# A hybrid encoder trunk: a head's eight groups of half-width products in one visit, and side work between the two products of a pair

## The chip, the cores and the metric

The kernel runs on one core of one Trainium2 chip. The metric is the device time of the whole program in microseconds (us), the median of several runs. The engines are named as the profile names them: PE (matrix products; PEld is its weight load), DVE (vector), ACT (scalar), POOL (general purpose), and SP, which issues most of the DMAs.

## The reference

The reference is a two-layer encoder trunk on 256 tokens of width 2048. Layer 0 mixes tokens with a bidirectional mLSTM, layer 1 with a bidirectional gated linear recurrence (HGRN2); each mixer is followed by a gated MLP of width 5504 with a convolution of width 3. The change touches the second mixer, whose core is this:

```python
def _hgrn_chunk(s_st, xs):
    q, k, lf, v = xs
    b = jnp.cumsum(lf, axis=2)
    rel = jnp.where(lower[:, :, None], b[:, :, :, None, :] - b[:, :, None, :, :], -jnp.inf)
    attn = jnp.einsum('bhtsk,bhsk->bhts', jnp.exp(rel) * q[:, :, :, None, :], k)
    o = jnp.einsum('bhts,bhsv->bhtv', attn, v) + jnp.einsum('bhtk,bhkv->bhtv', q * jnp.exp(b), s_st)
...
def hgrn_mixer(hn, w_in, lb, head_g, w_out):
    p = hn @ w_in
    q, i, g, f_f, f_b = jnp.split(p, [B_F, B_F + B_V, B_F + 2 * B_V, 2 * B_F + 2 * B_V], axis=-1)
    log_f = jnp.logaddexp(log_lb, log_1mlb + jax.nn.log_sigmoid(f))
    k = (1.0 - lb) * jax.nn.sigmoid(-f)
...
    y = hgrn_direction(q, k_f, lf_f, v) + fl(hgrn_direction(fl(q), fl(k_b), fl(lf_b), fl(v)))
    y = head_rmsnorm(y, head_g, B_HEADS) * jax.nn.silu(g)
    return y @ w_out
```

It has 16 heads of width 128. In words: a token's output is a sum over all earlier tokens (and, in the other direction, all later ones) of q times k times the product of the gates between the two tokens, times v.

## The kernel before

**The stream.** `stream` (line 151) runs through a list of chunks of weights. For each piece of 1024 columns `split_weights` has a DMA bring the float32 weights (`raw`), ACT round them to a high part `wh` (line 146) and DVE subtract to get the low part `wl` (line 147). Four buffers hold each part, and three pieces are prepared ahead. A chunk of kind "fm" has two output tiles f = 0, 1 and a contraction index k from 0 to 15 (or 21, 20); for each k and f there is a **pair** of products: `wh` against 512 columns (activations' high and low part, line 197) and `wl` against 256 columns (line 198). A chunk of kind "tm" has three products of 512 columns for each half of the tokens (lines 187 to 189). After each k the stream calls `side.tick`, with 0.65 units in "fm" and 1.3 in "tm".

**The side jobs.** `Side` (line 82) holds Python generators. A tick adds to a clock; a generator whose due time has come is run to its next `yield`, which names the units to the next step (2.4 for most heads of the second mixer, 1.9 for the last two and where nothing is named). The instructions that it issues thereby stand in program order at that tick. The framework that builds the program then lays out each engine's order by program order and by when its own model of times has the operands ready; an instruction whose operands are late moves behind others. Once built, each engine's order is fixed. A **visit** is a run of side products on PE between two products of the stream.

**A head of the second mixer.** `head` (line 596) waits until the head before it has set `done`, then goes through seven levels h = 1, 2, ..., 64. At each level DVE copies ("gathers") the blocks of k and q that matter there into two tiles `km` and `qm` of 256 columns (line 608), multiplies k and q by gates (lines 629, 630), and POOL multiplies neighbouring gates (line 635). Each level's tiles give one **group** of four half-width products (64 columns of weights, 64 columns streamed, line 616), and plain float32 takes two passes for each. An eighth group comes from `ks` and `q` (line 641). The groups fill quarters of a PSUM tile `pd`; with seven levels and one for `ks`, the eight groups take two tiles. Before the change they come in two visits: after level 4 (`li == 2`) the groups of levels 1, 2, 4 and of `ks`, whose results ACT copies (line 642) and DVE merges by mask (line 644) into `AD`; and after the last level the groups of levels 8 to 64, merged by line 650 and copied into `AT` (lines 654, 655), directly followed by two full-width products `pd<-QK` (lines 657, 658), copied by line 659. One step later AT meets V in eight products `py` (line 670). `done` is set in the second visit.

**Around it.** For every four heads there are three "fm" chunks, a "tm" chunk (V), three "fm" chunks and a "tm" chunk (the output gate). `finish` (line 677) scales four heads' outputs, transposes each on PE (`pz`, line 691) and writes them to `yb0` to `yb15`, in the buffers `yt0` to `yt15`, which the output projection reads. PSUM has four tiles for the stream and four (`aux`) for the side work. `km` and `qm` have five buffers each (`MIX`).

Of the kernel before, what the change touches and what calls it, by code (L numbers as in the profile page):

```python
# [8 lines left out]
F32 = mybir.dt.float32  # L9
# [6 lines left out]
P = 128  # L16
T = 256
D = 2048
KT = D // P
# [25 lines left out]
MIX = 5  # L45
FIRST = (0, 1, 2, 4, 7, 10, 13, 16)

HALF = 64
LEVELS = (1, 2, 4, 8, 16, 32, HALF)
# [4 lines left out]
def trunk_kernel(ctx, tc, xT, pp_d, cst_d, w_first, w_aq, w_ak, w_av, w_ao, w_aout,  # L54
                 w_bq, w_bv, w_bg, w_bout, w_up, w_down, out, mscr, stop=9):
    nc = tc.nc
    act, dve, pool, pe = nc.scalar, nc.vector, nc.gpsimd, nc.tensor

    keep = ctx.enter_context(tc.tile_pool(name="keep", bufs=1))
# [18 lines left out]
    def aux(name):  # L78
        return psa.tile([P, 512], F32, tag="aux", name=name)
# [30 lines left out]
    side = Side()  # L110
# [40 lines left out]
    def stream(chunks):  # L151
        pieces = split_weights(chunks)
        ready = []

        def fetch():
            p = next(pieces, None)
            if p is not None:
                ready.append(p)

        for _ in range(LOOK):  # L160
            fetch()
        for ch in chunks:
            if ch.before:
                ch.before()
            ps = [psm.tile([P, 512], F32, tag="mm", name="mm") for _ in range(3 if ch.kind == "first" else 2)]
            k = 0
            while k < ch.nk:
                fetch()
                wh, wl, n = ready.pop(0)
                if ch.last:  # L170
                    for f in range(2):
                        for kk in range(n):
                            x, c = ch.x(k + kk), kk * 256 + f * P
                            terms = ((wh, 0), (wl, 0), (wh, T))
                            for i, (w, o) in enumerate(terms):
                                pe.matmul(ps[f][:, 0:T], w[:, c:c + P], x[:, o:o + T], start=(k + kk == 0 and i == 0),  # L176
                                          stop=(k + kk == ch.nk - 1 and i == 2))
                    k += n
                    continue
                for kk in range(n):  # L180
                    x = ch.x(k)
                    st, sp = k == 0, k == ch.nk - 1
                    if ch.kind != "fm":
                        c = slice(kk * 512, (kk + 1) * 512)
                        for t in range(2):
                            xh, xl = x[:, t * P:(t + 1) * P], x[:, T + t * P:T + (t + 1) * P]
                            pe.matmul(ps[t], xh, wh[:, c], start=st, stop=False)  # L187
                            pe.matmul(ps[t], xh, wl[:, c], start=False, stop=False)  # L188
                            pe.matmul(ps[t], xl, wh[:, c], start=False, stop=sp)  # L189
                        if ch.kind == "first":  # L190
                            pe.matmul(ps[2], wh[:, 512:512 + P], x, start=st, stop=False)
                            pe.matmul(ps[2][:, 0:T], wl[:, 512:512 + P], x[:, 0:T], start=False, stop=sp)
                        side.tick(1.3)
                    else:
                        for f in range(len(ps)):
                            c = kk * ch.width + f * P
                            pe.matmul(ps[f], wh[:, c:c + P], x, start=st, stop=False)  # L197
                            pe.matmul(ps[f][:, 0:T], wl[:, c:c + P], x[:, 0:T], start=False, stop=sp)  # L198
                        side.tick(0.325 * len(ps))
                    k += 1  # L200
            ch.done(ps)

# [16 lines left out]
    def late(dst, src):  # L219
        tc.keep_in_program_order(nc.sync.dma_start(dst, src))  # L220
# [315 lines left out]
    def hgrn(norm, nxt):  # L536
        YT = [None] * KT
        stack = ExitStack()
        box = {}

        def begin():
            mp = box["mp"] = stack.enter_context(tc.tile_pool(name="hg", bufs=1))
            late(cst[:, C_LV:], cst_d[:, C_LV:])
            lb = box["lb"] = mp.tile([P, KT], F32, name="lb")
            oml = box["oml"] = mp.tile([P, KT], F32, name="oml")
            t0 = mp.tile([P, 2, KT], F32, name="t0")
            t1 = mp.tile([P, KT], F32, name="t1")
            raw = pp[:, OFF["lb"]:OFF["lb"] + 2 * KT].rearrange("p (a b) -> p a b", a=2)
            dve.tensor_tensor(t1, raw[:, 0], raw[:, 1], ALU.max)
            for i in range(2):  # L550
                dve.tensor_tensor(t0[:, i], raw[:, i], t1, ALU.subtract)
            act.activation(t0, t0, AF.Exp)
            dve.tensor_tensor(t1, t0[:, 0], t0[:, 1], ALU.add)
            dve.reciprocal(t1, t1)
            for i in range(2):
                dve.tensor_tensor(t0[:, i], t0[:, i], t1, ALU.mult)
            dve.tensor_tensor(lb, t0[:, 0], t0[:, 1], ALU.add)
            dve.tensor_tensor(lb, lb, t0[:, 0], ALU.subtract)
            dve.tensor_scalar(oml, lb, -1.0, 1.0, ALU.mult, ALU.add)

        def blocks(z, h, a, b):
            v = z[:, 0:2 * (T + h)].rearrange("k (p x) -> k p x", p=2)[:, :, a:b]
            return v.rearrange("k p (m j) -> k m p j", j=2 * h)[:, :, :, 0:h]

        def gview(g, n, start, h):
            v = g[:, start:start + 2 * (n - 1)].rearrange("k (p x) -> k p x", p=2)[:, :, 0::2]
            return v.rearrange("k p m -> k m p").unsqueeze(3).broadcast_to([P, n // 2, 2, h])
# [28 lines left out]
        def head(hd):  # L596
            mp = box["mp"]
            st = heads[hd]
            while hd and "done" not in heads[hd - 1]:
                yield 0.3  # L600
            QZ, KZ = st["QK"][:, 0:640], st["QK"][:, 512:1152]
            q, ks, G = st["q"], st["ks"], st["G"]
            AT = mp.tile([P, 4, P], F32, tag="AT", bufs=2, name="AT")
            AD = mp.tile([P, 2, HALF], F32, tag="AD", bufs=2, name="AD")

            def gather(z, h, tag):
                m = mp.tile([P, T], F32, tag=tag, bufs=MIX, name=tag)
                dve.tensor_copy(m.rearrange("k (m p j) -> k m p j", p=2, j=h), blocks(z, h, 0, T))
                return m

            def product(pd, k, q, flip=0):

                for b in range(4):
                    o, c = b % 2 * HALF, b // 2 * HALF
                    e = b ^ flip
                    pe.matmul(pd[o:o + HALF, c:c + HALF], k[:, b * HALF:(b + 1) * HALF], q[:, e * HALF:(e + 1) * HALF],  # L616
                              start=True, stop=True)

            def both(ps):
                return ps.rearrange("p (a b) -> p a b", a=2)  # L620

            step = SPREAD if hd < BH - 2 else STEP
            mask = [cst[:, C_LV + i * HALF:C_LV + (i + 1) * HALF].bitcast(I32).unsqueeze(1).broadcast_to([P, 2, HALF])
                    for i in range(6)]
            ms, n = [(gather(KZ, 1, "km"), gather(QZ, 1, "qm"))], T
            yield step
            for li, h in enumerate(LEVELS):
                qa, ka = blocks(QZ, h, 0, T), blocks(KZ, h, 0, T)
                dve.tensor_tensor(ka, ka, gview(G, n, 1, h), ALU.mult)  # L629
                dve.tensor_tensor(qa, qa, gview(G, n, n + 1, h), ALU.mult)  # L630
                if h < HALF:
                    ms.append((gather(KZ, 2 * h, "km"), gather(QZ, 2 * h, "qm")))
                    n //= 2
                    G2 = mp.tile([P, 3 * n], F32, tag=f"G{h}", bufs=2, name="G2")
                    pool.tensor_tensor(G2, G[:, 0:6 * n:2], G[:, 1:6 * n:2], ALU.mult)
                    G = G2
                if li == 2:
                    pd = aux("pd")
                    for i in (2, 1, 0):
                        product(pd[:, (i + 1) * P:(i + 2) * P], *ms[i])  # L640
                    product(pd[:, 0:P], ks, q)
                    act.copy(AD, both(pd[:, 0:P]))
                    for i in range(3):
                        dve.copy_predicated(AD, mask[i], both(pd[:, (i + 1) * P:(i + 2) * P]))
                yield step
            pd = aux("pd")
            for i in (6, 5, 4, 3):
                product(pd[:, (i - 3) * P:(i - 2) * P], *ms[i], i == 6)
            for i in (3, 4, 5):
                dve.copy_predicated(AD, mask[i], both(pd[:, (i - 3) * P:(i - 2) * P]))  # L650
            src = both(pd[:, 3 * P:4 * P])
            st["done"] = True
            for o in (0, HALF):
                act.copy(AT[o:o + HALF, 0::3, HALF - o:P - o], src[o:o + HALF])
                act.copy(AT[o:o + HALF, 0::3, o:o + HALF], AD[o:o + HALF])
            pd = aux("pd")
# [6 lines left out]
            V, j = st["qd"]["V"], hd % 4  # L663
# [229 lines left out]
```

## Time and profile before

| what | number |
|---|---|
| median of 3 runs | 2452.22 us (2452.00 to 2452.59) |
| the profiled execution's own time | 2451.01 us |
| its span, first to last instruction | 2449.2 us |
| granted PE clock, mean | 0.998 |
| second mixer with its projection, by the windows view | 1150 to 1664 us |
| in that stretch: PE, DVE, ACT, POOL busy | 512.8, 438.1, 263.2, 129.2 us of 514 |
| half-width products (line 616), records | 896 + 128 |

The table's stretch of 514 us is the only part of the program in which the heads of the second mixer run. A PE record begins when PE starts on a matmul and ends when its last result is out; records overlap, so the distance from one start to the next is what a matmul takes of PE's time, not the record's length. The timeline merges equal neighbours into one line: the first column is the start of the first, the second the time to the end of the last, and the count stands behind x.

### The profile page before, as it was taken

The page shows a single profiled execution, that of the slowest core. Times are in us where ns is not written, and L with a number is a line of the kernel's source. Part 1 is how long each engine was busy: PE and PEld are TensorE (multiplying, and loading weights), DVE is VectorE, ACT ScalarE, POOL GpSimd, SP SyncE. Part 2 cuts the span into 40 slices and gives each one's busy share as a digit, 9 for nine tenths or more (in the row PEclk, how much of TensorE's full clock was granted, in tenths as well). Part 3 has the DMA queues.
Part 4 walks back from the last instruction along what each step waited for, and adds up shares of the span by engine and source line. Part 5 has one row for each costly group of instructions (what it writes and reads, how often), then busy time and mean ns, then how long its engine had stood idle before and what let it go on. Part 6 is the DMA issues. An engine that isn't in the chain of part 4 may idle for free.

```text
span 2449.2 us, 36986 instructions
## 1 busy us (share of the span) xinstructions
PE 2432.1 (99%) x14462; PEld 2108.3 (86%) x14462; DVE 1759.7 (72%) x2943; ACT 1221.2 (50%) x1890; POOL 267.4 (11%) x325
## 2 busy tenths in 40 slices
PE   9999999999999999999999999999999999999998
PEld 7888888888888888888888888888888888888887
DVE  7766577777656777668888888888777755677754
ACT  6655455444444444445455555545544444444443
POOL 0100032000000000122222222224000000000022
PEclk9999999999999999999999999999999999999999
DMA  7654555555556555555544445445555555555553
GB/s 261 189 179 160 184 187 184 191 191 191 179 189 202 189 189 189 181 183 191 172 160 168 162 165 172 160 156 201 186 191 191 186 189 194 189 189 189 185 190 125
DMA packets 65920, 448.88 MB, mean 183 GB/s; under 512 B 7616, under 2 KB 8256, under 8 KB 15568
## 3 DMA queue, kind: packets, MB, share of 16 engines
q1 hardware_dynamic: 63936, 443.03, 54.2%
q0 software_dynamic: 800, 2.16, 0.6%
q8 instruction: 113, 1.85, 0.3%
q10 hardware_dynamic: 1008, 1.32, 0.2%
q14 instruction: 63, 0.52, 0.1%
HBM read 444.32 MB, written 2.16 MB: 182 GB/s over the span
## 4 chain that ended last, share of the span: by engine, by line
PE 98%; DVE 1%; ACT 0%; issue 0%; DMA 0%; SPq 0%; POOL 0%; DVEq 0%; POOLq 0%
PE mm L197 53%; PE mm L198 26%; PE mm L187 5%; PE mm L189 5%; PE mm L188 5%; PE pd L616 1%; PE pn L440 1%; PE mm L176 1%; PE py L670 1%; DVE wl L147 0%; PE S L426 0%; PE pd L657 0%; DMA raw<-in_w_first 0%; DVE QK L629 0%; PE pz L691 0%
## 5 line engine op out<-in xcount | busy, mean ns | idle before, releaser
L147 DVE TENSOR_TENSOR wl<-raw,wh 128x1024 fp32r<-128x1024 f32 (+1 forms) x864 | 1047.5, 1214 | 546.4 <-ACT wh L146 533.5
L197 PE MATMUL mm<-xt,wh 128*128 128x512 f32 x3776 | 1319.5, 395 | 0.0
L146 ACT CAST wh<-raw 128x1024 fp32r<-128x1024 f32 (+1 forms) x864 | 884.1, 1025 | 833.2 <-PE mm L197 481.5
L198 PE MATMUL mm<-xt,wl 128*128 128x256 f32 x3776 | 1049.9, 278 | 0.0
L197 PEld LDWEIGHTS mm<-xt,wh 128*128 128x128 f32 x3776 | 708.3, 188 | 164.3
L198 PEld LDWEIGHTS mm<-xt,wl 128*128 128x128 f32 x3776 | 710.1, 188 | 0.8
L197 PE MATMUL mm<-g,wh 128*128 128x512 f32 x1334 | 462.6, 394 | 0.0
L198 PE MATMUL mm<-g,wl 128*128 128x256 f32 x1334 | 369.5, 277 | 0.0
L197 PEld LDWEIGHTS mm<-g,wh 128*128 128x128 f32 x1334 | 250.1, 188 | 58.0
L198 PEld LDWEIGHTS mm<-g,wl 128*128 128x128 f32 x1334 | 250.5, 188 | 0.0
L187 PE MATMUL mm<-wh,xt 128*128 128x512 f32 x512 | 201.9, 398 | 3.1 <-ACT xt L204 2.5
L188 PE MATMUL mm<-wl,xt 128*128 128x512 f32 x512 | 201.5, 394 | 0.4 <-DVE wl L147 0.4
L189 PE MATMUL mm<-wh,xt 128*128 128x512 f32 x512 | 200.6, 393 | 0.0
L209 ACT COPY b<-mm 128x256 f32<-128x256 f32 x237 | 87.6, 370 | 172.2 <-PE mm L198 172.2
L243 POOL TENSOR_TENSOR acc<-hx 128x256 f32<-128x256 f32 x4 | 4.8, 1203 | 1238.3 <-DVE hx L312 1238.3
L187 PEld LDWEIGHTS mm<-wh,xt 128*128 128x128 f32 x512 | 95.7, 188 | 23.3 <-ACT xt L204 2.7
L189 PEld LDWEIGHTS mm<-wh,xt 128*128 128x128 f32 x512 | 96.5, 188 | 19.9
L188 PEld LDWEIGHTS mm<-wl,xt 128*128 128x128 f32 x512 | 96.5, 188 | 19.4 <-DVE wl L147 0.8
L197 PE MATMUL mm<-yb,wh 128*128 128x512 f32 x256 | 89.6, 396 | 0.0
L197 PE MATMUL mm<-ya,wh 128*128 128x512 f32 x256 | 89.1, 394 | 0.0
L246 POOL TENSOR_TENSOR sq<-hx 128x256 f32<-128x256 f32 x52 | 62.7, 1214 | 193.4 <-DVE hx L312 191.2
L210 DVE TENSOR_TENSOR a<-mm,b 128x256 f32<-128x256 f32 x86 | 36.5, 425 | 50.9 <-ACT b L209 50.7
(188 smaller groups left out, 1999.2 us busy)
## 6 DMA issues: line engine op xcount, KB each, us to landing
raw<-in_w_up SPq DMA_DIRECT2D x172, 1024.0 KB, 4.9
raw<-in_w_down SPq DMA_DIRECT2D x64, 1024.0 KB, 4.8
raw<-in_w_bq SPq DMA_DIRECT2D x48, 1024.0 KB, 4.9
raw<-in_w_ao SPq DMA_DIRECT2D x16, 1024.0 KB, 4.9
raw<-in_w_aout SPq DMA_DIRECT2D x16, 1024.0 KB, 4.9
raw<-in_w_bv SPq DMA_DIRECT2D x16, 1024.0 KB, 4.9
raw<-in_w_bg SPq DMA_DIRECT2D x16, 1024.0 KB, 4.9
raw<-in_w_bout SPq DMA_DIRECT2D x16, 1024.0 KB, 4.9
```

The costliest lines, as they stand in the source:

```text
L146: act.copy(wh[:, :m], r)
L147: dve.tensor_tensor(wl[:, :m], r, wh[:, :m].bitcast(F32), ALU.subtract)
L176: pe.matmul(ps[f][:, 0:T], w[:, c:c + P], x[:, o:o + T], start=(k + kk == 0 and i == 0), stop=(k + kk == ch.nk - 1 and i == 2))
L187: pe.matmul(ps[t], xh, wh[:, c], start=st, stop=False)
L188: pe.matmul(ps[t], xh, wl[:, c], start=False, stop=False)
L189: pe.matmul(ps[t], xl, wh[:, c], start=False, stop=sp)
L197: pe.matmul(ps[f], wh[:, c:c + P], x, start=st, stop=False)
L198: pe.matmul(ps[f][:, 0:T], wl[:, c:c + P], x[:, 0:T], start=False, stop=sp)
L209: act.copy(b, ps[:, T:2 * T])
L210: dve.tensor_tensor(dst, ps[:, 0:T], b, ALU.add)
L246: eng.tensor_tensor(s, hT[k], hT[k], ALU.mult)
L440: pe.matmul(pn[:, 0:258], w, v, start=(i == 0), stop=(i == len(parts) - 1))
```

## The change

It has two parts. In the stream, the tick of an "fm" step moves from behind both pairs to between the two products of the second pair (f = 1). In the second mixer, the visit at `li == 2` goes away: all eight groups are issued in one visit after the last level, into two PSUM tiles, with the copy into `AD` and all six masked merges after them. To hold seven levels' operands till then, k and q of a level share one tile of 2 x 256 columns, and there are nine such tiles in turn: four in the buffers `yt12` to `yt15`, five (`MIX`) of their own. `done` is set at the last level, one step before the visit.

```diff
                             pe.matmul(ps[f], wh[:, c:c + P], x, start=st, stop=False)
+                            if f:
+                                side.tick(0.325 * len(ps))
                             pe.matmul(ps[f][:, 0:T], wl[:, c:c + P], x[:, 0:T], start=False, stop=sp)
-                        side.tick(0.325 * len(ps))
...
+            def gather(h):
+                i = box["turn"] % (4 + MIX)
+                box["turn"] += 1
+                if i < 4:
+                    m = keep.tile([P, 2, T], F32, tag=f"yt{KT - 4 + i}", name=f"kq{i}")
+                else:
+                    m = mp.tile([P, 2, T], F32, tag="kq", bufs=MIX, name="kq")
+                for j, z in enumerate((KZ, QZ)):
+                    dve.tensor_copy(m[:, j].rearrange("k (m p j) -> k m p j", p=2, j=h), blocks(z, h, 0, T))
+                return m[:, 0], m[:, 1]
...
-                if li == 2:
-                    pd = aux("pd")
-                    for i in (2, 1, 0):
-                        product(pd[:, (i + 1) * P:(i + 2) * P], *ms[i])
-                    product(pd[:, 0:P], ks, q)
-                    act.copy(AD, both(pd[:, 0:P]))
-                    for i in range(3):
-                        dve.copy_predicated(AD, mask[i], both(pd[:, (i + 1) * P:(i + 2) * P]))
+                if h == HALF:
+                    st["done"] = True
                 yield step
-            pd = aux("pd")
-            for i in (6, 5, 4, 3):
-                product(pd[:, (i - 3) * P:(i - 2) * P], *ms[i], i == 6)
-            for i in (3, 4, 5):
-                dve.copy_predicated(AD, mask[i], both(pd[:, (i - 3) * P:(i - 2) * P]))
-            src = both(pd[:, 3 * P:4 * P])
-            st["done"] = True
+            pds = [aux("pd") for _ in range(2)]
+            part = [pds[i // 4][:, i % 4 * P:(i % 4 + 1) * P] for i in range(8)]
+            for i in reversed(range(7)):
+                product(part[i + 1], *ms[i], LEVELS[i] == HALF)
+            product(part[0], ks, q)
+            act.copy(AD, both(part[0]))
+            for i in range(6):
+                dve.copy_predicated(AD, mask[i], both(part[i + 1]))
+            src = both(part[7])
```

More of the change, by code (lines that the diff above doesn't have):

```diff
@@ L543, in begin @@
             late(cst[:, C_LV:], cst_d[:, C_LV:])
+            box["turn"] = 0
             lb = box["lb"] = mp.tile([P, KT], F32, name="lb")
@@ L604, in head @@
             AD = mp.tile([P, 2, HALF], F32, tag="AD", bufs=2, name="AD")
[L606 to L609, printed above, removed]
+            def gather(h):
[8 more added lines that the diff above has]
+                return m[:, 0], m[:, 1]
             def product(pd, k, q, flip=0):
@@ L624, in head @@
                     for i in range(6)]
-            ms, n = [(gather(KZ, 1, "km"), gather(QZ, 1, "qm"))], T
+            ms, n = [gather(1)], T
             yield step
@@ L631, in head @@
                 if h < HALF:
-                    ms.append((gather(KZ, 2 * h, "km"), gather(QZ, 2 * h, "qm")))
+                    ms.append(gather(2 * h))
                     n //= 2
```

## The prediction

> **What bounds the kernel.** I read the page first, then PE's waits, then PE's timeline around the side visits of the second mixer, start by start.
>
> ```profile
> PE 2432.1 (99%) x14462; PEld 2108.3 (86%) x14462; DVE 1759.7 (72%) x2943; ACT 1221.2 (50%) x1890; POOL 267.4 (11%) x325
> ...
> PE 98%; DVE 1%; ACT 0%; issue 0%; DMA 0%; SPq 0%; POOL 0%; DVEq 0%; POOLq 0%
> ```
>
> PE is busy 99% of the span and makes 98% of the chain that ended last. In the waits of PE only one of the second mixer reaches 0.5 us, that of the first head:
>
> ```profile
> PE pd L616 <- DVE qm L608: 0.8, 1, 0.8
> ```
>
> So nothing shortens the time but fewer or cheaper PE slots, and anything else counts only if it comes late to PE. Now PE's timeline, head 5's first visit, in a "tm" chunk:
>
> ```profile
> 1302.63 0.39 PE L188 MATMUL mm<-wl,xt 128*128 128x512 f32 x1
> 1302.86 0.39 PE L189 MATMUL mm<-wh,xt 128*128 128x512 f32 x1
> 1303.17 0.92 PE L616 MATMUL pd<-qm,km 128*64 128x64 f32 x24
> 1303.92 0.40 PE L616 MATMUL pd<-q,ks 128*64 128x64 f32 x8
> 1304.26 0.50 PE L187 MATMUL mm<-wh,xt 128*128 128x512 f32 x1
> 1304.59 0.39 PE L188 MATMUL mm<-wl,xt 128*128 128x512 f32 x1
> ```
>
> Look at the starts. A product of the stream takes 0.227 (0.23 in the rows). The one before the visit takes 0.31, the first after it 0.33. The stream pays 0.09 to enter half-width products, and at the way out 0.15 from the last half-width start to L187 and 0.11 more before L188. The second visit, in an "fm" chunk:
>
> ```profile
> 1319.22 0.28 PE L198 MATMUL mm<-xt,wl 128*128 128x256 f32 x1
> 1319.43 1.15 PE L616 MATMUL pd<-qm,km 128*64 128x64 f32 x32
> 1320.51 0.49 PE L657 MATMUL pd<-QK 128*128 128x128 f32 x2
> 1320.84 0.39 PE L658 MATMUL pd<-QK 128*128 128x128 f32 x2
> 1320.98 0.48 PE L197 MATMUL mm<-xt,wh 128*128 128x512 f32 x1
> 1321.29 0.28 PE L198 MATMUL mm<-xt,wl 128*128 128x256 f32 x1
> ```
>
> It pays its own entry (0.206 where a `wl` otherwise takes 0.117: 0.09) and its own way out, into L657.
>
> **Part 1, the merged visit.** The first visit from L189's start to L188's takes 1.73; two ordinary steps would be 0.454, so it costs 1.28 us. Its 32 records inside: the 24 of the first row take 0.75, of which the first pair of passes 0.10; the other eleven pairs take 0.65, or 0.059 each (0.058 in the single starts). Appended to a run of half-width products that is open anyway, 16 such pairs cost 16 x 0.058 = 0.93. Each head saves 1.28 - 0.93 = 0.35 us. All 16 first visits have these starts (1.400 or 1.486 from last to first product of the stream; the 0.086 belongs to the `py` visit just before). **16 x 0.35 = -5.6 us**. Bounds: at best the second tile's products also spare the settling of the stream after a visit (about 0.03 each): -6.1. At worst a second tile costs another first pair of 0.10 instead of 0.058: -4.9.
>
> **What it adds off PE.** Counts stay: 224 gathers, 96 masked merges, 16 copies of line 642, 96 gate products on POOL; no DMA is added or moved past a queue. What moves is the copy (0.25) and three merges (0.30 each) of a head, from the middle to the end, in front of AT and `py`. I cost it at nothing, since the end of AT's copies (line 654) is ahead of `py`: 1236.65 against 1238.65 for head 2, 1322.87 against 1326.36 for head 5, and alike for all even (2.0 us, or 7.4 where V is late) and odd heads (3.5 us). Three merges of head 4 stand at 1299.37, 1300.10 and 1300.84, one each 0.73 us with the next head's work between them; three more add 2.2 us, with the copy 2.4, so an even head's cover of 2.0 would be short by 0.4 if PE's order stayed as it is. Eight heads, four of them with the long cover: 0 to 4 x 0.4 = 1.6 us. I take nothing, as the order is laid out anew with the longer chain in it. Queued behind the merges on DVE are weight splits (line 147); matched one by one to the first `wl` product that reads them, they are done 3.4 us or more ahead in the second mixer, except around head 0 (1.4). A burst of 0.9 us fits.
>
> **The earlier `done`** lets a waiting head begin one step earlier, so its first gathers (0.3 each) and gate products (0.42 each) queue on DVE behind level 64's multiplies and ahead of the merges: cost nothing by the same cover. **Buffers**: nine pairs of operands where a head needs seven; the third gather of the next head is the first to wait for this head's visit, two steps (over 4 us) after the visit's due time. The two `pd` tiles, the QK tile and `py` take four `aux` buffers per head as before. At the end `yb12` to `yb15` share buffers with the last head's operands, so they wait for its products, which stood at 1632.24; their transposes stood at 1631.1 to 1646.9, while PE worked on a second chunk of the projection. Cost 0 to 1 us, taken as 0.
>
> **Head 0.** Its second visit waited 0.87 us for the last gather (1.19 from L189 to the visit instead of 0.32). Without three merges (0.89) before that gather, it comes earlier; the visit may be placed earlier too. 0 to -0.9: I take -0.4.
>
> **Part 2, the tick.** Entering costs the same after either product: 0.09 for half-width products after a 256- or a 512-column product, 0 to 0.01 for full-width ones. But the stream's beat afterwards differs. After `py`, which left into `wh`:
>
> ```profile
> 1327.60 0.39 PE L197 MATMUL mm<-xt,wh 128*128 128x512 f32 x1
> ...
> 1328.66 0.40 PE L197 MATMUL mm<-xt,wh 128*128 128x512 f32 x1
> ```
>
> Three pairs, 1.06 us: 0.3533 a pair. After transposes that left into `wl`:
>
> ```profile
> 1397.64 0.38 PE L691 MATMUL pz<-cst,y 128*128 128x128 f32 x2
> 1397.78 0.36 PE L198 MATMUL mm<-xt,wl 128*128 128x256 f32 x1
> 1397.98 0.40 PE L197 MATMUL mm<-xt,wh 128*128 128x512 f32 x1
> ...
> 1399.37 0.40 PE L197 MATMUL mm<-xt,wh 128*128 128x512 f32 x1
> ```
>
> Four pairs, 1.39 us: 0.3475 by these rounded rows, 0.3467 over the whole stretch in single starts. The beat holds until the next visit. Going through all starts, nine of nine stretches that begin behind an exit into `wl` have the short beat; behind `py` and QK exits, which all led into `wh`, all but one have the long one. Against a simple rule: the norm's column sums left into `wh` and still gave the short beat, and no `py` or QK exit into `wl` exists. Per four heads, 24 + 14 + 44 + 14 + 17 = 113 pairs run long behind such exits, about 436 in all: 436 x 0.0067 = 2.9 us if all turn short. The QK visits stand at ticks (whole k), so they move between the products; 28 pairs per four heads follow them (0.75 us in all). `py` comes when AT is ready, not at a tick; I count half of the other 2.2 us, and three chances in four that the beat follows the exit: (0.75 + 1.1) x 0.75 = **-1.4**; bounds 0 and -2.9, and up to +1.1 if stretches now short (some 170 pairs) turn long.
>
> **Sum.** -5.6 - 0.4 - 1.4 = -7.4 us: 2451.01 - 7.4 = 2443.6 for the profiled execution (span 2449.2, 1.8 around it). That execution lies 1.2 below the median shown; the median after is 2452.2 - 7.4 = **2444.8 us**. A measurement of this kernel can tell 0.2%, 4.9 us.
>
> **Rivals.** *Merge alone pays* (2446.2): the beat stays long and only 5.6 + 0.4 is saved. For it: entry costs 89 ns after `wl` and 91 after a 512-column product, so place seems not to matter. The Trainium skill, "TensorEngine Tiling (Array Packing)", section Key Properties, says that changing the array's tiling mode drains the engine, a cost by the number of changes and not by place; the trace agrees with the 0.09. *The visits of even heads wait for data* (2451.2): their gate products for QK end only 0.5 to 0.9 us before L657, and head 0 waited 0.87; if the next head's earlier start pushes them back, eight heads by 0.8 eat 6.4 of the 7.4 us. Against it: sixteen more pairs of passes now stand between the visit's start and L657 (0.93 us more cover). *`py` comes late* (slower, 2462.8): if the copy and the three more merges end AT 4.5 us later (over 1 us each, where head 4's stand 0.73 apart), the four heads with 2.0 us of cover wait 2.5 each and the eight odd heads 1.0 each: +18 - 7.4 = +10.6. It outweighs the gain from a delay of 3.6 us on (4 x 1.6 + 8 x 0.1 = 7.2), if the laid-out order does not allow for it; the 2.4 us worked out above and DVE's 15% of idle time in the mixer speak against it. *Not what it says* (2452): the eight groups are laid out in pieces, as head 15's visit was, around two transposes.
>
> **Chances.** Forecast 0.53, merge alone 0.21, even heads wait 0.13, `py` late 0.09, pieces 0.04. Below 2447.3 lie nearly all of the first two: faster 0.73, same 0.18, slower 0.09. The likeliest case's own range is 2441.5 (6.1 + 0.9 + 2.9, and a little) to 2447.5 (4.9 saved); taking in most of the waiting cases, 2440 to 2451.
>
> **What would show it.** Right: 64 half-width and 4 QK records in each of 16 visits, and no visit halfway through a head; entry still 0.09, exit unchanged; QK visits in "fm" between L197 and L198, followed by 0.3467 a pair; PE's waits on DVE below 1 us in all. Wrong: a row of PE waits on `kq` gathers, QK or AT of several us; a long beat behind exits into `wl`; half-width pairs above 0.06 us.

## The result and the profile after

The changed kernel takes 2463.14 us (median of 5 runs, 2462.14 to 2463.95) against 2452.22 us; the ratio is 1.0044 with a 95% interval of 1.0032 to 1.0056. It is slower by 10.9 us where 7.4 us less were forecast. The profiled execution took 2463.62 us, its span is 2461.9 us, 12.7 more than before.

The page's busy times and its chain of waits, after:

```profile
PE 2444.0 (99%) x14462; PEld 2116.2 (86%) x14462; DVE 1765.2 (72%) x2943; ACT 1219.1 (50%) x1890; POOL 279.1 (11%) x325
...
PE 93%; DVE 5%; issue 1%; ACT 1%; DMA 0%; SPq 0%; POOL 0%; DVEq 0%; ACTq 0%; POOLq 0%
```

PE has the same 14462 matmuls and is busy 11.9 us longer. It does not wait much more. These are PE's waits after (total us, times, longest), with only the rows of the second mixer:

```profile
PE pd L625 <- DVE kq L617: 1.1, 1, 1.1
...
PE pz L696 <- DVE y L690: 0.9, 3, 0.4
...
PE py L675 <- ACT AT L660: 0.5, 2, 0.2
```

So the loss has to be in the distance between matmuls. It is found by going through the stages, and it is not in the second mixer at all. The view by windows (length; then busy us and matmuls that touch the window for PE, PEld, DVE, ACT, POOL; clock, DMA share, GB/s), for 680 us inside the first MLP, before:

```profile
444.00:1124.00 680.00, 680.00 (x3925) 594.66 (x3925) 468.60 (x706) 326.55 (x465) 26.86 (x27) 1.00 0.57 191
```

and after:

```profile
444.00:1124.00 680.00, 680.00 (x3851) 590.03 (x3850) 458.88 (x686) 318.43 (x454) 26.39 (x27) 1.00 0.56 186
```

PE is fully busy in both, at full clock, and nobody is waited for; but 74 fewer matmuls pass. Two matmuls are a pair: 680 / 3925 x 2 = 0.3465 us before, 680 / 3851 x 2 = 0.3532 us after. These are the two beats of the prediction, and the whole first MLP, in which no side job runs and the moved tick has nothing to move, has gone from the short one to the long one. (The Trainium skill, "Perfetto Trace Analysis", section Identifying the Most-Contended Engine, warns that PE's matmul busy share does not tell how near to its limit PE is and names the share of the matmul peak and the weight load's busy time as better measures. The trace agrees in part: PE's 680.00 is the same and PEld's falls from 594.66 to 590.03, but by 0.8% where the matmuls fall by 1.9%.)

I went through the starts of all pairs and added up what each takes above 346.67 ns, leaving out pairs over 370 ns (those with a visit's exit in them):

| stage | before | after | difference, us |
|---|---|---|---|
| first mixer | 1.57 | 1.50 | -0.1 |
| first MLP, with the end of the projection before it | 0.00 | 15.50 | +15.5 |
| second mixer | 3.46 | 1.56 | -1.9 |
| rest of its projection, second MLP | -0.01 | 1.27 | +1.3 |

The beat alone makes +14.8 us, more than the whole difference of the spans. Late starts of visits in the second mixer (over the usual entry) grow from 2.2 to 4.5 us, +2.3; the merged visits give -5.5 (below). Together +11.6 of the 12.7; 1.1 us are not accounted for.

**Where the beat is set.** PE's timeline at the end of the first mixer, before. Four transposes `pz` stand behind a pair; then the pairs of the projection; at 322.26 the framework's layout has put two high products next to each other, at the border of two chunks:

```profile
317.55 0.28 PE L198 MATMUL mm<-ya,wl 128*128 128x256 f32 x1
317.66 0.60 PE L468 MATMUL pz<-cst,y 128*128 128x128 f32 x4
318.02 0.47 PE L197 MATMUL mm<-ya,wh 128*128 128x512 f32 x1
...
322.26 0.63 PE L197 MATMUL mm<-ya,wh 128*128 128x512 f32 x2
...
324.01 0.40 PE L197 MATMUL mm<-ya,wh 128*128 128x512 f32 x1
```

The same place after. The moved tick puts the transposes between the two products, and PE goes on with the low one:

```profile
317.03 0.40 PE L197 MATMUL mm<-ya,wh 128*128 128x512 f32 x1
317.27 0.60 PE L469 MATMUL pz<-cst,y 128*128 128x128 f32 x4
317.62 0.36 PE L200 MATMUL mm<-ya,wl 128*128 128x256 f32 x1
...
321.98 0.63 PE L197 MATMUL mm<-ya,wh 128*128 128x512 f32 x2
...
323.74 0.40 PE L197 MATMUL mm<-ya,wh 128*128 128x512 f32 x1
```

Up to the double high product both run short, before as 347, 346, 347, after as 351, 342, 351, 342 ns. Behind it the kernel before stays short (350, 344, 350, 343); the changed one runs 350, 361, 349, 351, 360, 349, the long beat, and keeps it for 2310 pairs, up to 1143 us. The experiments ask whether this is the cause, and what turns a beat. None of them moves the last transposes alone: that it is they, and not another visit of the first mixer, is read off this timeline.

### The profile page after: what moved, and what is told of

Its sections match the earlier page's. It is cut to its first block, busy times and chain, and to the rows that moved or that the text cites. A ratio compares the mean times of both kernels' runs of the same rounds, so it can differ in the third digit from the quotient of the medians.

```text
span 2461.9 us, 36944 instructions
## 1 busy us (share of the span) xinstructions
PE 2444.0 (99%) x14462; PEld 2116.2 (86%) x14462; DVE 1765.2 (72%) x2943; ACT 1219.1 (50%) x1890; POOL 279.1 (11%) x325
## 3 DMA queue, kind: packets, MB, share of 16 engines
HBM read 444.32 MB, written 2.16 MB: 181 GB/s over the span
## 4 chain that ended last, share of the span: by engine, by line
PE 93%; DVE 5%; issue 1%; ACT 1%; DMA 0%; SPq 0%; POOL 0%; DVEq 0%; ACTq 0%; POOLq 0%
PE mm L197 52%; PE mm L200 26%; PE mm L188 3%; PE mm L187 3%; PE mm L189 3%; DVE wl L147 2%; PE pd L625 1%; DVE QK L638 1%; DVE kq L617 1%; PE pn L441 1%; DVE QK L639 1%; PE mm L176 1%; PE py L675 0%; PE S L427 0%; ACT wh L146 0%
## 5 line engine op out<-in xcount | busy, mean ns | idle before, releaser
L197 PE MATMUL mm<-xt,wh 128*128 128x512 f32 x3776 | 1326.4, 397 | 0.0
L200 PE MATMUL mm<-xt,wl 128*128 128x256 f32 x3776 | 1056.8, 280 | 0.0
L197 PEld LDWEIGHTS mm<-xt,wh 128*128 128x128 f32 x3776 | 709.7, 188 | 167.9
L200 PEld LDWEIGHTS mm<-xt,wl 128*128 128x128 f32 x3776 | 712.8, 189 | 1.2
L197 PE MATMUL mm<-g,wh 128*128 128x512 f32 x1334 | 467.2, 397 | 0.0
L200 PE MATMUL mm<-g,wl 128*128 128x256 f32 x1334 | 372.6, 279 | 0.0
L197 PEld LDWEIGHTS mm<-g,wh 128*128 128x128 f32 x1334 | 250.7, 188 | 60.4
L200 PEld LDWEIGHTS mm<-g,wl 128*128 128x128 f32 x1334 | 251.7, 189 | 0.0
L197 PE MATMUL mm<-yb,wh 128*128 128x512 f32 x256 | 90.7, 400 | 0.0
L197 PE MATMUL mm<-ya,wh 128*128 128x512 f32 x256 | 90.5, 399 | 0.0
```

## The experiments

The theory: in "fm" stretches PE keeps one of two beats, 346.7 or 353.3 ns a pair, until something foreign or out of order passes; the moved tick changed what passes at the end of the first mixer, and the first MLP inherits it. The rival: the merged visit, its buffers or its waits make the kernel slower.

| run | median, us | beside it, before | ratio (95%) |
|---|---|---|---|
| e1, merge alone | 2448.34 | 2452.24 | 0.9984 (0.9975 to 0.9994) |
| e2, tick alone | 2466.68 | 2452.24 | 1.0059 (1.0044 to 1.0074) |
| e3, tick moved in the second mixer only | 2447.57 | 2452.24 | 0.9981 (0.9972 to 0.9991) |
| e4, useless products, into the low product | 2455.51 (one run) | 2452.24 | |
| f1, the same in the kernel before, into the high one | 2469.94 (one run) | 2452.12 | |
| f2, swapped order in ten steps | 2456.80 (one run) | 2452.12 | |
| f4, e3 with the late `done` | 2447.57 | 2452.12 | 0.9982 (0.9972 to 0.9991) |
| g1, the changed kernel with two swaps | 2448.63 | 2451.38 | 0.9988 (0.9979 to 0.9996) |
| g2, e3 with swaps in the first mixer | 2446.90 | 2451.38 | 0.9979 (0.9970 to 0.9988) |
| h1, g2 with a later `py` | 2446.67 | 2451.35 | 0.9980 (0.9971 to 0.9989) |
| h2, the kernel before with one swap | 2452.13 | 2451.35 | 1.0003 (0.9994 to 1.0012) |
| h3, the same swap, further on | 2465.49 | 2452.45 | 1.0053 (1.0036 to 1.0069) |

**e1, the merge alone.** The changed kernel with the tick back:

```diff
-                            if f:
-                                side.tick(0.325 * len(ps))
                             pe.matmul(ps[f][:, 0:T], wl[:, c:c + P], x[:, 0:T], start=False, stop=sp)
+                        side.tick(0.325 * len(ps))
```

> The merged visit with the tick back behind both pairs. Theory (the beat of the stream decides: the moved tick changed the visits in the first mixer's tail, and so the beat that the first MLP keeps for 2310 pairs): the first mixer's PE order is that of the kernel before, so the first MLP runs at 346.7 ns a pair again, the 15.5 us go, and the merge keeps what it saved less its new waits: 2444 to 2451 us. Rival (the merge itself, with its new waits and buffers, makes the kernel slower): 2460 us or more, with the first MLP unchanged at 353.3 ns.

2448.34 us: the merge makes the kernel faster, and the rival falls. The first MLP's excess over the short beat is 0.0 us. In the second mixer the QK visits leave into the high product, as in the kernel before, and yet behind six of the eight in "fm" chunks the beat is short.

**e2, the tick alone.** The kernel before with the opposite edit.

> The kernel before with only the tick moved. Theory: the first mixer's tail is that of the changed kernel, so the first MLP keeps the long beat of 353.3 ns a pair from about 323 us on: +15 us there, -1 to -3 us in the second mixer, 2462 to 2468 us in all. Rival (the merge is what costs): at most 2453 us.

2466.68 us, slower than the changed kernel, which has both parts. Excess in the first MLP 15.5 us, in the second mixer 2.4 instead of 3.5. The whole loss belongs to the moved tick. Here the QK visits leave into the low product, and behind five of those eight the beat is long.

**e3, the tick moved in the second mixer only.** The changed kernel with

```diff
-                            if f:
+                            if f and ch.mid:
                                 side.tick(0.325 * len(ps))
                             pe.matmul(ps[f][:, 0:T], wl[:, c:c + P], x[:, 0:T], start=False, stop=sp)
+                        if not ch.mid:
+                            side.tick(0.325 * len(ps))
...
         c = hgrn(n2, n3)
+        for ch in c:
+            ch.mid = True
```

> The changed kernel, but the tick stands between the products only in the chunks of the second mixer and its projection; in the first mixer it stands behind both pairs. Theory: first MLP at the short beat (346.7 ns), second mixer as in the changed kernel, 2463.1 - 15.5 = 2447.6 us, and up to 1.3 us less if the second MLP's first 180 pairs turn short too. Rival (the long beat in the first MLP comes from elsewhere, such as where the buffers lie): about 2463 us.

2447.57 us, as worked out. Excess in the first MLP 0.0, in the second mixer 1.7, behind it 0.0. So it is the tick in the first mixer that costs. In the second mixer it gains a little by the traces: from the first half-width product to the last transpose e3 takes 474.1 us and e1 474.6. The medians of the two do not tell this apart.

**e4, useless products.** The changed kernel, with this between the two products of the second pair, at k = 8 of every sixth chunk of the first MLP:

```diff
+    def poke(kind):
+        t = aux("poke")
+        if kind == 2:
+            for b in range(4):
+                o, c = b % 2 * HALF, b // 2 * HALF
+                pe.matmul(t[o:o + HALF, c:c + HALF], ones[:, 0:HALF], ones[:, 0:HALF], start=True, stop=True)
+            for c in (P, 2 * P):
+                pe.matmul(t[:, c:c + P], ones[:, 0:P], ones[:, 0:P], start=True, stop=True)
+        else:
+            pe.matmul(t[:, 0:P], ones[:, 0:P], ones[:, 0:P], start=True, stop=True)
```

> The changed kernel with useless products in the first MLP, in every sixth chunk at k = 8, between the two products of the second pair: by turns one full-width float32 product (two passes), and four half-width ones with two full-width ones. Their results go nowhere. Theory: the beat changes at such places and nowhere else in the MLP; after the second kind, which ends like the second mixer's merged visits that left into the low product (seven of seven followed by the short beat), it is 346.7 ns till the next poke. With half of the pairs turned short, some 7 us are won against 0.3 to 0.6 us for each of about ten pokes: 2459 to 2464 us, and the beat's two values side by side in one stage. Rival (place of buffers, memory traffic of the stage): all pairs stay at 353.3 ns, 2466 to 2469 us.

2455.51 us. The first poke, of the plain kind, was enough. PE's timeline there:

```profile
441.29 0.40 PE L208 MATMUL mm<-xt,wh 128*128 128x512 f32 x1
...
442.00 0.39 PE L208 MATMUL mm<-xt,wh 128*128 128x512 f32 x1
442.24 0.38 PE L160 MATMUL poke<-ones 128*128 128x128 f32 x2
442.37 0.36 PE L213 MATMUL mm<-xt,wl 128*128 128x256 f32 x1
442.57 0.40 PE L208 MATMUL mm<-xt,wh 128*128 128x512 f32 x1
...
444.32 0.39 PE L208 MATMUL mm<-xt,wh 128*128 128x512 f32 x1
```

Two pairs from 441.29 to 442.00 take 0.71, then five from 442.57 to 444.32 take 1.75: 0.350 with the pair that settles, 0.347 from there on. Behind all ten pokes the beat is short, and it stays so for the remaining 700 us. By the single starts a plain poke costs 0.22 us and one of the other kind 1.0, so the ten cost 6 us, the upper end of what the expectation counted. Only the first poke met a long beat; the nine behind it met a short one and left it.

**f1, the same pokes with PE going on into the high product**, in the kernel before, whose first MLP is short:

> The kernel before (first MLP at the short beat) with the same useless products in every sixth chunk of the first MLP, but behind both pairs, so that PE goes on with a high product. Theory A (which product comes next decides: into the low one short, into the high one long): the pokes turn the MLP long, 353.3 ns a pair behind most of them, 2452.2 + 10 to 17 us = 2462 to 2469. Theory B (any disturbance draws the beat anew, the product that follows does not decide): some stretches long, some short, by the kind of poke; 2455 to 2462. Rival (a beat that runs short stays short whatever comes): 2.2 to 4 us for the ten pokes alone, 2454.4 to 2456.

2469.94 us, a little above theory A's range since the ten pokes cost some 6 us together. The first two left the beat short, the third turned it long at 575 us, and after the other seven it was long: 10.7 us in the MLP, 1.4 behind it. Those seven met a long beat and left it, where e4's plain poke into the low product had turned one at once; but of the three that met a short beat only one turned it. So which product follows a poke matters at most in part: 10 of 10 exits into the low product were followed by the short beat and 8 of 10 into the high one by the long, and all but two of these 18 by the beat that was there already.

**f2, a swap without any added work**, in the changed kernel:

```diff
+                    elif ch.poke and k == 8:
+                        for w, m, last in ((wh, 2 * T, False), (wl, T, sp)):
+                            for f in range(2):
+                                c = kk * ch.width + f * P
+                                pe.matmul(ps[f][:, 0:m], w[:, c:c + P], x[:, 0:m], start=st, stop=last)
```

> The changed kernel (first MLP at the long beat) without any added product: in every sixth chunk of the first MLP, at k = 8, the four products of the step run in the order high, high, low, low instead of high, low, high, low. Theory: the order of weight loads against the stream sets the beat, so a swap with no added work can turn it too; if the first swap turns it, some 14 us are won, 2449; if it turns at a later one, correspondingly less. Rival (only a foreign product, in plain float32, turns it): 2462 to 2464 us, all of the MLP at 353.3 ns.

2456.80 us, and the trace is the plainest of all: at each of the ten swaps the beat turns over, long to short at 442, back to long at 508, short at 576, and so on. The first MLP's excess is 8.4 us instead of 15.5. No foreign product is needed; the order of PE's own products does it.

**f4, the late `done`.**

```diff
-                if h == HALF:
+                if h == HALF and hd >= 12:
                     st["done"] = True
...
             src = both(part[7])
+            st["done"] = True
```

> As e3 (tick moved in the second mixer alone), but for heads 0 to 11 the mark that lets the next head begin is set behind the visit again. In e3 the py and pz products of the second mixer wait 2.9 us more than in the kernel before (late starts of py by 0.2 to 0.4 and of pz by 0.3 to 0.5 us, twice to four times each). Theory (the next head's gathers, which start one step earlier, stand among the six merges on DVE and make AT and y late): the waits of the first three groups of four heads go, 0.7 us each, 2445.5 us. Rival (the six merges alone make them late): 2447.6 us as e3, with py and pz as late as there.

2447.57 us, the rival's figure. `py` starts late by 0.2 to 0.4 us four times (1.3 in all) and `pz` by 0.3 to 0.5 four times (1.7), as in e3, where the two make the expectation's 2.9. The earlier `done` is not what delays them. What remains are the six merges behind the visit, but no run took them apart, so this part of the cause is argued and not shown. (In the profiled runs of f4 and h1, but not in those of e3 and g2, the second MLP's first 180 pairs ran long, which is 1.2 us. So equal medians alone would not show that nothing was gained; the late starts do.)

**g1, two swaps in the changed kernel**, at k = 8 of the fourth chunk of each mixer's projection (`tail[3].swap = 8`, the step as in f2).

> The changed kernel, with one step's products in the order high, high, low, low at k = 8 of the fourth chunk of each mixer's projection, where the long beat begins: two steps in all, no work added or taken away. Theory (the beat is a state that a swap turns over and that then holds): from about 360 us to the end of the first MLP 346.7 ns a pair, some 2200 pairs x 6.7 ns = 14.7 us, and 160 pairs or 1.1 us ahead of the second MLP; 2463.1 - 15.8 = 2447.3 us. Rival (the beat drifts back by itself in some chunk): anything from 2449 to 2463 us, with the place of the return in the trace.

2448.63 us. The first swap, at 350.5 us, turned the beat, and with that the first MLP is short to its end: excess 0.5 instead of 15.5. A swap reorders four of 14462 matmuls and adds none; the two take back 14.5 of the 15.8 us hoped for (13.7 if each kernel is taken against the kernel before measured beside it). The second, at 1665.0 us, left the beat long (1.05 us behind it). The two differ in their place in the long beat's cycle of three pairs, whose high products take 241, 236 and 233 ns: the first fell on a place of 232, the second on one of 236. Of all swaps that I placed in a long beat, eight fell on 240 or 241 and turned it.

**g2, e3 with such a swap at k = 1 of the first mixer's q chunks.**

> e3 (tick moved in the second mixer alone) with such a swap at k = 1 of the q chunks of the first mixer, where the stretches of 63 pairs ran long. Theory: three stretches of about 60 pairs turn short, 1.2 us, and the first MLP stays short since its beat is drawn in the tail behind them: 2446.4 us. Rival (the swap turns what is short, such as the first of the four stretches, or the tail draws another beat): 2447.6 to 2449 us, or 2463 us if the first MLP turns long.

2446.90 us against 2451.38: the lowest ratio here, though e3, f4 and h1 lie within its interval (h1's median is 0.2 us lower). The first mixer's excess falls from 1.57 to 0.34 us.

**h1, a later `py`** (`yield 2 * STEP` behind the copies into AT, in the kernel of g2).

> The kernel of g2 with the py products of a head issued 3.8 units after its AT copies instead of 1.9. Theory (PE meets py before the six merges on DVE have let ACT finish AT): the late starts of py, 1.2 us in all, go, those of pz stay: 2445.7 us. Rival (py comes later but so does everything behind it, or a beat is drawn anew): 2446.9 us or up to 1.5 us to either side of it.

2446.67 us: no gain. `py` starts as late as before (0.2, 0.2, 0.4 and 0.4 us), and for all heads but the last it stands at the same product of the stream as in g2, so its place does not come from the tick. That the layout's model, which places it by when AT is ready, sets it is argued. This expectation was wrong.

**h2 and h3, one swap in the kernel before.** h2 has `tail[3].swap = 8` in the first mixer alone.

> The kernel before, with nothing changed but the order of four products of one step: high, high, low, low at k = 8 of the fourth chunk of the first mixer's projection. Theory: the short beat turns long there and holds through the first MLP, some 2200 pairs x 6.7 ns = 14.7 us: 2466 to 2467 us. Rival (the beat is a matter of the mixers' side work and returns by itself): 2452 to 2455 us.

2452.13 us, against the expectation. The swap did turn the beat long at 350 us, but the norm's column sums at 410 us turned it short again: 1.1 us in the stage instead of 14.7. So in h3 the swap stands behind them, in the fourth chunk of the MLP (`c[3].swap = 8`).

> The kernel before with one step's products in the order high, high, low, low at k = 8 of the fourth chunk of the first MLP (about 440 us), behind the norm's products, which turned the beat back in h2 at 410 us. Theory: in f2 all five swaps that met the short beat turned it long, and nothing but chunks of pairs follows till the norm at 1130 us: some 1980 pairs x 6.7 ns = 13.2 us, 2452 + 13 = 2465 us. Rival (something in the MLP turns it back, as the norm did): less, with the place in the trace; 2452 us if at once.

2465.49 us, 13.0 more than beside it. PE's timeline at the swap:

```profile
439.24 0.40 PE L203 MATMUL mm<-xt,wh 128*128 128x512 f32 x1
439.47 0.28 PE L204 MATMUL mm<-xt,wl 128*128 128x256 f32 x1
439.59 0.62 PE L198 MATMUL mm<-xt,wh 128*128 128x512 f32 x2
440.04 0.40 PE L198 MATMUL mm<-xt,wl 128*128 128x256 f32 x2
440.28 0.40 PE L203 MATMUL mm<-xt,wh 128*128 128x512 f32 x1
...
441.34 0.40 PE L203 MATMUL mm<-xt,wh 128*128 128x512 f32 x1
```

and the windows view of the same 680 us as above:

```profile
444.00:1124.00 680.00, 680.00 (x3851) 589.64 (x3851) 458.70 (x684) 318.33 (x454) 26.77 (x27) 1.00 0.56 186
```

The swapped step itself takes 0.69 us (439.59 to 440.28), as any other. Behind it three pairs take 1.06 us, and the count over 680 us is that of the changed kernel, 3851. The kernel before has become as slow as the changed one by the order of four matmuls. Together with e2 and e3 that settles the cause: the moved tick in the first mixer sets the long beat, and the long beat costs the time.

## Why the prediction was wrong, point by point

**The step that failed** is the tick's. The prediction priced it at -1.4 us, with "up to +1.1 if stretches now short (some 170 pairs) turn long", and counted the second mixer's stretches only. But the edit is in `stream`, and its tick serves the first mixer as well. The transposes at the end of that mixer moved too; the beat that they leave behind turned long at the double high product 4.7 us later, and is held not for a few dozen pairs but through the first MLP. The same two beats and the same 6.7 ns, applied to the 2310 pairs of that MLP and some 180 ahead of the second, give +16.6 us as the term's upper end, and the range would have reached to about 2463 (2446.2 without the tick, and 16.6). That there are two beats and that they are held had been read off the trace; the list of places where this counts was not complete, and the rule for what sets a beat did not hold either (below).

**What came near by luck.** *The beat in the second mixer*: the stage's excess fell by 1.9 us, where -1.4 was forecast, but not by the rule behind the term, that the beat follows the product into which a visit leaves. The QK visits in "fm" chunks do leave into the low product now, and behind seven of the eight the beat is plainly short (five pairs follow the last); that is 0.6 us. The larger part, 2.0, stands behind `py`, which leaves into the high product as before: of the eleven stretches of six or more pairs behind it, ten are now short, where all eleven were long. Head 5's, in the prediction 1.06 us for three pairs, after:

```profile
1338.51 1.05 PE L675 MATMUL py<-V,AT 128*128 128x128 f32 x8
...
1339.75 0.40 PE L197 MATMUL mm<-xt,wh 128*128 128x512 f32 x1
...
1340.79 0.39 PE L197 MATMUL mm<-xt,wh 128*128 128x512 f32 x1
```

Three pairs take 1.04 us. Some single transposes, which now leave into the high product, add 0.6 us of long beat. With e1 and e2, where most QK exits were followed by the other beat than the rule says, the rule is refuted; what decides the beat behind a visit stays open.

**What held.** *The merged visit.* PE's timeline of one, after:

```profile
1328.57 0.40 PE L197 MATMUL mm<-xt,wh 128*128 128x512 f32 x1
1328.89 1.85 PE L625 MATMUL pd<-kq 128*64 128x64 f32 x56
1330.58 0.40 PE L625 MATMUL pd<-q,ks 128*64 128x64 f32 x8
1330.91 0.49 PE L662 MATMUL pd<-QK 128*128 128x128 f32 x2
1331.23 0.39 PE L663 MATMUL pd<-QK 128*128 128x128 f32 x2
1331.38 0.36 PE L200 MATMUL mm<-xt,wl 128*128 128x256 f32 x1
```

From L197 to L200 2.81 us, less the ordinary 0.23: 2.58. The second visit before took 1.76 less 0.12, 1.64. The 32 added records cost 0.94, where 0.93 was worked out, and the first visit's 1.28 is gone: 0.34 us a head, 5.5 in all. Entry still costs 0.09 (0.32 instead of 0.23). Of the 16 heads only the last has its visit cut up, by transposes. (Its first visit before was no plain case either: it stood in one with a `py` visit, 2.29 us from product to product of the stream, where the prediction gives 1.40 or 1.49 for all 16.)

**What was mis-sized.** *Work off PE at nothing*: `py` of each group's third head (1.2 us) and the first transposes `pz` behind it (1.7) start late, by 2.9 us in all. One such `py`, after, with the head's last masked merge and the first copy into AT, which starts as that merge ends:

```profile
1255.46 0.30 DVE L656 COPY_PREDICATED AD<-cst,pd 128x128 f32<-128x128 int32 x1
...
1255.80 0.26 ACT L659 COPY AT<-pd 64x128 f32<-64x128 f32 x1 [3.38 <-DVE AD L656]
...
1256.89 1.16 PE L675 MATMUL py<-V,AT 128*128 128x128 f32 x8
```

And PE's timeline of one such `pz`:

```profile
1385.56 0.40 PE L197 MATMUL mm<-xt,wh 128*128 128x512 f32 x1
1386.31 0.30 PE L696 MATMUL pz<-cst,y 128*128 128x128 f32 x1 [0.36 <-DVE y L690]
```

0.75 us from L197 to the transpose instead of 0.23: the product waits for DVE to scale y. I had looked for the delay at `py` alone (bounds 0 to 1.6 us; 1.2 measured) and not at what DVE does next. *Head 0*: -0.4 was taken; the visit now starts 1.2 us late instead of 0.9, but QK behind it no longer waits (0.5), so -0.2. The merge with these waits gives 3.9 us (e1, in which the second MLP's first 180 pairs also turned long, 1.2 us).

**The rivals.** "Merge alone pays" is nearest to e1 and was right in that place does not change the cost of entering. The reason that I gave for it, the drain at a change of the array's mode in the Trainium skill, "TensorEngine Tiling (Array Packing)", section Key Properties, says nothing of the beat afterwards, and it is there that the tick's place counted (excess in the first MLP 0.0 in e1, 15.5 after). "`py` comes late" happened in small, with 1.2 us instead of 18; that its 2462.8 lies near the measured 2463.14 is chance. None of them was the cause.

## What to carry to other kernels

An edit in a helper that all stages call is to be priced in all of them, also where no line of the stage is changed: compare the same stretch of every stage before and after, by matmuls per microsecond and not by PE's busy time. Where PE is the bound and its stream is regular, look at the distances between starts for more than one beat; if there are two, a change of a few instructions far upstream can be worth more than the work that the edit removes. The order of a step's products is then a thing to try for itself, since it adds no work.

## What the runs showed of the hardware

With float32r weights loaded for each product, alternating products of 512 and 256 columns run at 346.7 or at 353.3 ns a pair, at the same clock, with nobody waited for and no difference in the instructions. A beat holds from pair to pair, in the changed kernel for over 800 us, from 324 to 1143. A long one was turned by a plain float32 product ahead of a low product (e4's first poke, the only one so placed that met a long beat); a short one by one of f1's three pokes ahead of a high product that met it. Either was turned by the order high, high, low, low (7 of 7 swaps placed in a short beat turned it long, 9 of 10 placed in a long one turned it short; one of g2's stood among other products and is not counted) and a long one, at some places, by a norm's column sums (in h2 at 410 us; after, at the same place, not). Which product follows a visit does not decide the beat: behind `py`, always into the high product, 11 of 11 stretches of six or more pairs were long before and 10 of 11 are short after. A short beat of the form 347, 346, 347 survived a double high product at 322 us, one of the form 351, 342 did not. What turns a beat at one place and not at another, and what in PE sets the two values, stays open: no run looked below the starts of matmuls and weight loads.
